# SSD scan: output transposes one period behind the norm, step-size transposes behind the fifth unit, four output rows split ahead of the last unit

## The chip, the core and the metric

The kernel runs on one core of a Trainium2 chip. A core has TensorE (PE in the profile) for matmuls and transposes, VectorE (DVE), ScalarE (ACT) and GpSimd (POOL) for elementwise work, and SyncE (SP), whose queue issues every transfer of this kernel. Each engine takes its instructions strictly in the order in which they stand in its queue, and waits at each one until its semaphores allow it. The metric is the device time of one execution in microseconds (us); lower is better.

## What is computed

The program is a stack of layers over 1024 tokens of width 1024. The change lies in the second mixer, a state space layer (SSD), and in the layernorm behind it:

```
z, xbc, dt = split(x @ w_in)                     # 2048 + 3072 + 32 columns
xbc = silu(causal_conv4(xbc));  xs, B, C = split(xbc)      # 4 groups, state 128
dt = softplus(dt + dt_bias);  a = -exp(a_log)
cs = cumsum(dt * a) in chunks of 128 tokens
y_diag = ((C B^T) * exp(cs_l - cs_s), lower triangle) @ (xs * dt)
state  = B^T (xs * dt * exp(cs_end - cs)), carried from chunk to chunk
y = y_diag + (C @ state) * exp(cs) + d_skip * xs
y = rmsnorm over a group of 512 of (y * silu(z)), * norm_w
out = y @ w_out                                  # 2048 -> 1024
x = layernorm(sqrt2 * x + out);  then rmsnorm(x) feeds the feed-forward layer
```

All matmuls take fp32 operands split in a high and a low part (`whi`, `wlo`; `x` holds both parts of the activations), three products for each.

## The kernel before, in words

The SSD layer's input projection is cut into four groups of ten units on TensorE. In a group, units 0 and 1 (`states`) give B and C, units 2 to 5 (`inputs`) give x, 48 matmuls of 128x512 each (L174); units 6 to 9 (`gates`) give z, 96 matmuls of 128x256 (L860 to L862). A unit's weights come by one or two transfers into `wst` (L156), are rounded to `whi` on ScalarE (L140) and completed by `wlo` on VectorE (L141). Behind the first six units the result goes through a causal convolution: ScalarE copies it out of PSUM (L331, L332), VectorE adds three taps (L334).

The scan of group g runs while the units of group g+1 run: behind each of its first eight units stands one chunk of 128 tokens (`chunk(n)`, n = 8g to 8g+7), that of the last group behind the eight tiles of the output projection. I call a unit with its chunk a period. A chunk is
- `heads(n)`: eight small matmuls (L916), their sum on VectorE (L917);
- `between(n)`: the carried state (L925, L930, L926 to L933); the transfer of the gate values into `xw` (L936);
- `within(n+1)`: the next chunk's decay matrix `s` (transfer L897, GpSimd L898, VectorE L899, ScalarE L900, VectorE L909), B C^T (L902, L903), and three products on GpSimd (L906 to L908);
- `finish(n-1)`: the gate product (L941), the sum of squares (ScalarE L943), the inverse root in nine small VectorE steps (tiles `rs`, L259 to L269), the scaling (ScalarE L945), four transposes into PSUM (L948), the copy out (ScalarE L949) and the transfer to memory (L950).

Ahead of the first group stand the step sizes: `lead` (L191) multiplies the dt columns and the first unit together, `softplus` and the cumulative sum run on VectorE (to L796), and seven TensorE instructions (L807 to L812) turn the result round for the scan.

Behind the fourth group `SsdOut` computes y @ w_out. `fill(k)` loads, scales and splits one of 16 rows of w_out (L1003, ScalarE L1005, VectorE L1006). `early(i)` multiplies rows 8, 9 and 0 to 7 for token tile i (60 matmuls, L668); `rest()` multiplies the other six rows (36 matmuls) and runs the layernorm (L1066, then L653 to L659) and the next layer's rmsnorm (L1081 to L1091) on the tile. Each second tile `ops.build` transposes both tiles (16 transposes, L1137) and forms the operands of the feed-forward layer, whose matmuls are L1230.

What sets the order: the Tile framework schedules instructions into the engines' queues from the order in which they are written and from its own costs. `turn()` is `issue_after(anchor(K))`: what is written in it stands behind the last TensorE instruction written so far. Buffers are rings: two for `wst`, four each for `whi` and `wlo` (the copy `raw` for the convolution takes one of the `wlo` ring too), two for the large PSUM tiles `pa`, four for the small ones `pb`. A tile takes the slot of the one as many allocations before it, and waits until that one's last reader is done.

## Time and profile before

| | |
|---|---|
| three runs, median (lowest to highest) | 3383.68 us (3379.7 to 3386.35) |
| profiled execution: its time, its span | 3383.42 us, 3381.6 us |
| mean granted TensorE clock | 0.963 |
| busy: PE, DVE, ACT, POOL | 3093.0 (91%), 2281.6 (67%), 1623.7 (48%), 779.2 us (23%) |

The profiled execution lies 0.26 us from the median, so its rows can be read for the median. 1.8 us of its time lie outside the span. A row of the timeline gives start, duration, engine, line of the program, operation, what it writes and reads by tile name, and in brackets how long the engine had been idle before it and what ended that. The granted clock of TensorE has two levels in these rows, 1.00 (2.4 GHz) and 0.50 (1.2 GHz).

### The profile page before, as it was taken

What the parts mean: (1) busy time and instruction counts of PE and PEld (TensorE: products, weight loads), DVE (VectorE), ACT (ScalarE), POOL (GpSimd) and SP (SyncE); (2) the same over time, 40 slices, a digit from 0 to 9 for tenths busy, and PEclk for the clock granted to TensorE, in tenths of its full rate; (3) what the DMA queues carried; (4) which work ended last, traced back from release to release, by engine and by line L of the source; (5) the groups of instructions that cost most, each with busy time, mean ns of one, the idle gap of its engine ahead of it and who ended that gap; (6) DMA issues with size and microseconds to landing.
All of it is one profiled execution on the core that took longest, in us unless ns stands there. A gap on an engine that the chain in (4) does not pass through costs nothing. (4 is left out here: it accounts for less than half of the span.)

```text
span 3381.6 us, 42341 instructions
## 1 busy us (share of the span) xinstructions
PE 3093.0 (91%) x15560; PEld 2582.5 (76%) x15560; DVE 2281.6 (67%) x3819; ACT 1623.7 (48%) x2943; POOL 779.2 (23%) x487
## 2 busy tenths in 40 slices
PE   8999996999999889878999989899999699999997
PEld 6878875878787867667778877678787588888776
DVE  6537775366657555888785689835676955555998
ACT  5526533345545532465555434542475665554442
POOL 0000011113232211532233345100000423232543
PEclk9999998999999999989999999999999899999999
DMA  3257342233343555323332620435453422224322
GB/s 126 66 198 222 105 142 66 63 82 103 88 115 82 141 177 159 102 77 131 112 116 85 213 83 22 156 126 211 137 154 127 163 75 78 90 76 142 113 81 112
DMA packets 344960, 398.99 MB, mean 118 GB/s; under 512 B 20656, under 2 KB 270640, under 8 KB 344752
## 3 DMA queue, kind: packets, MB, share of 16 engines
q1 hardware_dynamic: 344752, 396.28, 37.5%
q8 instruction: 123, 2.02, 0.2%
q14 instruction: 85, 0.70, 0.1%
HBM read 279.29 MB, written 116.92 MB: 117 GB/s over the span
## 5 line engine op out<-in xcount | busy, mean ns | idle before, releaser
L141 DVE TENSOR_TENSOR wlo<-wst,whi 128x1024 fp32r<-128x1024 f32 (+1 forms) x190 | 225.5, 1190 | 338.9 <-ACT whi L140 338.7
L174 PE MATMUL pa<-x,whi 128*128 128x512 f32 x1568 | 430.5, 396 | 5.2 <-ACT l L332 2.7
L140 ACT ACTIVATE whi<-wst 128x1024 fp32r<-128x1024 f32 (+1 forms) x190 | 180.0, 949 | 355.9 <-PE pa L174 94.0
L174 PEld LDWEIGHTS pa<-x,whi 128*128 128x128 f32 x1568 | 294.3, 189 | 69.8 <-issue 3.4
L147 ACT ACTIVATE wst<-wst,pk 128x128 f32<-128x128 f32 (+1 forms) x816 | 251.5, 391 | 177.8 <-DMA wst<-in_ffn_w_in_dram 105.6
L174 PE MATMUL pa<-x,wlo 128*128 128x512 f32 x784 | 244.1, 393 | 1.8 <-DVE wlo L141 1.8
L1230 PE MATMUL pa<-x,whi 128*128 128x512 f32 (+1 forms) x736 | 222.6, 385 | 6.3 <-DVE rl L264 3.2
L1230 PE MATMUL pb<-x,whi 128*128 128x512 f32 (+1 forms) x736 | 224.0, 381 | 0.0
L1309 PE MATMUL pa<-wlo,whi 128*128 128x512 f32 x768 | 190.9, 407 | 15.5 <-DVE wlo L141 13.3
L1309 PE MATMUL pb<-wlo,whi 128*128 128x512 f32 x744 | 180.1, 400 | 13.8 <-DVE wlo L141 13.8
L1309 PEld LDWEIGHTS pa<-wlo,whi 128*128 128x128 f32 x768 | 151.0, 198 | 52.9 <-DVE wlo L141 17.7
L1193 POOL TENSOR_TENSOR s<-wst 128x512 f32<-128x512 f32 x44 | 57.6, 1310 | 570.7 <-ACT wst L147 532.0
L1309 PEld LDWEIGHTS pb<-wlo,whi 128*128 128x128 f32 x744 | 143.1, 193 | 46.6 <-DVE wlo L141 16.7
L174 PEld LDWEIGHTS pa<-x,wlo 128*128 128x128 f32 x784 | 148.0, 189 | 34.0 <-DVE wlo L141 2.2
L1230 PEld LDWEIGHTS pa<-x,whi 128*128 128x128 f32 x736 | 137.7, 192 | 34.1 <-issue 3.6
L1230 PEld LDWEIGHTS pb<-x,whi 128*128 128x128 f32 x736 | 135.8, 188 | 26.5 <-issue 0.4
L898 POOL TENSOR_TENSOR s<-s,p 128x1024 f32<-128x1024 f32 x32 | 63.8, 1995 | 382.5 <-DMA s<-d 382.5
L860 PE MATMUL pa<-whi,x 128*128 128x256 f32 x512 | 148.7, 290 | 1.6 <-ACT l L332 1.3
L861 PE MATMUL pa<-wlo,x 128*128 128x256 f32 x512 | 147.4, 288 | 0.0
L862 PE MATMUL pa<-whi,x 128*128 128x256 f32 x512 | 147.4, 288 | 0.0
L140 ACT ACTIVATE whi<-s 128x1024 fp32r<-128x1024 f32 x88 | 93.1, 1058 | 108.2 <-POOL s L1194 53.1
L1230 PE MATMUL pa<-x,wlo 128*128 128x512 f32 (+1 forms) x368 | 141.2, 385 | 0.1
(580 smaller groups left out, 8021.6 us busy)
## 6 DMA issues: line engine op xcount, KB each, us to landing
wst<-in_ffn_w_in_dram SPq DMA_DIRECT2D x88, 512.0 KB, 3.8
d<-l SPq DMA_DIRECT2D x83, 512.0 KB, 3.3
d<-p SPq DMA_DIRECT2D x82, 512.0 KB, 3.3
x<-d SPq DMA_DIRECT2D x128, 256.0 KB, 5.4
p<-d SPq DMA_DIRECT2D x46, 512.0 KB, 5.0
wst<-in_s_w_in_dram SPq DMA_DIRECT2D x40, 512.0 KB, 4.0
s<-d SPq DMA_DIRECT2D x32, 512.0 KB, 9.9
l<-d SPq DMA_DIRECT2D x24, 512.0 KB, 5.6
```

The lines of the kernel that those rows point to most:

```text
L140: K.nc.scalar.activation(hi, src, AF.Copy)
L141: (eng or K.nc.vector).tensor_tensor(lo, src, hi.bitcast(F32), ALU.subtract)
L147: K.nc.scalar.activation(st[:, k, :], st[:, k, :], AF.Copy, scale=col(K, gain, k0 + k))
L174: K.nc.tensor.matmul(ps[:, h:h + 512], w, x[:, h:h + 512], start=k == 0 and m == 0, stop=k == n - 1 and m == 2)
L860: nc.tensor.matmul(o, xh, wh, start=k == 0, stop=False)
L861: nc.tensor.matmul(o, xh, wl, start=False, stop=False)
L862: nc.tensor.matmul(o, xl, wh, start=False, stop=k == NK - 1)
L898: nc.gpsimd.tensor_tensor(mv, mv, per_head(csT, P), ALU.subtract)
L1193: G(s1, a21, a22, ALU.add)
L1230: nc.tensor.matmul(p, l[:, k, :], r[:, k, :], start=k + m == 0, stop=k == 3 and m == 2)
L1309: nc.tensor.matmul(bank[j], th[:, a + o:a + o + P], tw[:, b:b + 512], start=c + m == 0, stop=c == n - 1 and m == 2)
```

## The change

Five things are different.
1. The seven TensorE instructions of the step sizes and the copies behind them become a function `steps()`, called behind unit 4 of the first group.
2. `finish(n)` is cut in two. `norm(n)` stays where it was, one period behind its chunk. `flip(n)` (the transposes, the copy, the transfer to memory) goes one period later, to the head of `chunk(n+2)`; the copy goes into `xw` and no longer into `xdt`. On GpSimd the product `y` goes ahead of `xw`. A group's last two flips stand behind its units 8 and 9 (`close`), those of the last group behind the first two tiles of `rest`. `within` of a group's first chunk stands behind unit 8 and no longer behind unit 9.
3. Rows 8, 9, 0 and 1 of w_out are filled in `ahead()`, written behind unit 7 of the last group; rows 0 and 1 lie in two tiles `p` and no longer in `x`.
4. In `rest` each tile's matmuls are written under `issue_after` of the last TensorE instruction.
5. `rest` drives the last group's `close`.

```diff
@@ -801,17 +801,19 @@
         sl = slice(128 * c, 128 * c + 128)
         nc.scalar.activation(w2[:, sl], cs[:, sl], AF.Exp, bias=cs[:, 128 * c + 127:128 * c + 128], scale=-1.0)
     nc.vector.tensor_tensor(w2, w2, dt, ALU.mult)
-    b, b2 = K.B(), K.B()
-    for c in range(2):
-        sl = slice(128 * c, 128 * c + 128)
-        nc.tensor.transpose(b[:, 128 * c:128 * c + 128], dt[:, sl], K.ident)
-        nc.tensor.transpose(b[:, 256 + 128 * c:384 + 128 * c], cs[:, sl], K.ident)
-        nc.tensor.transpose(b2[:, 128 * c:128 * c + 128], w2[:, sl], K.ident)
-    nc.vector.tensor_copy(sf[:, 0:512], b)
-    nc.vector.tensor_copy(w2T, b2[:, 0:256])
-    nc.tensor.matmul(b2[:, 256:512], sel, csT, start=True, stop=True)
-    nc.scalar.activation(ecs, csT, AF.Exp)
-    nc.scalar.activation(cdb, b2[:, 256:512], AF.Exp)
+
+    def steps():
+        b, b2 = K.B(), K.B()
+        for c in range(2):
+            sl = slice(128 * c, 128 * c + 128)
+            nc.tensor.transpose(b[:, 128 * c:128 * c + 128], dt[:, sl], K.ident)
+            nc.tensor.transpose(b[:, 256 + 128 * c:384 + 128 * c], cs[:, sl], K.ident)
+            nc.tensor.transpose(b2[:, 128 * c:128 * c + 128], w2[:, sl], K.ident)
+        nc.vector.tensor_copy(sf[:, 0:512], b)
+        nc.vector.tensor_copy(w2T, b2[:, 0:256])
+        nc.tensor.matmul(b2[:, 256:512], sel, csT, start=True, stop=True)
+        nc.scalar.activation(ecs, csT, AF.Exp)
+        nc.scalar.activation(cdb, b2[:, 256:512], AF.Exp)
 
 
 
@@ -904,8 +906,8 @@
         nc.vector.tensor_tensor(cbm, b[:, 0:128], tri, ALU.mult)
         nc.scalar.activation(bt, b[:, 128:256], AF.Copy)
         nc.gpsimd.tensor_tensor(hv(xdt), hv(X), per_head(dtT, 64), ALU.mult)
+        nc.gpsimd.tensor_tensor(hv(y), hv(X), dsk[:, 8 * g:8 * g + 8].unsqueeze(2).to_broadcast([P, 8, 64]), ALU.mult)
         nc.gpsimd.tensor_tensor(hv(xw), hv(X), per_head(w2T, 64), ALU.mult)
-        nc.gpsimd.tensor_tensor(hv(y), hv(X), dsk[:, 8 * g:8 * g + 8].unsqueeze(2).to_broadcast([P, 8, 64]), ALU.mult)
         nc.vector.tensor_tensor(mv, mv, cbm.unsqueeze(1).to_broadcast([P, 8, P]), ALU.mult)
         held[n] = mv, Cc, xdt, xw, y, bt
 
@@ -935,54 +937,75 @@
                 nc.vector.tensor_copy(prev, st)
         nc.sync.dma_start(xw, sz_d[g][c * P:(c + 1) * P, :])
 
-    def finish(n):
-        g, c = divmod(n, 8)
-        _, _, xdt, sz, y, _ = held.pop(n)
+    def norm(n):
+        _, _, xdt, sz, y, _ = held[n]
         nc.vector.tensor_tensor(y, y, sz, ALU.mult)
         t = K.small(2, "yss", bufs=3)
         nc.scalar.activation(xdt, y, AF.Square, accum_out=t[:, 0:1])
         rsqrt_col(K, t[:, 1:2], t[:, 0:1], 1, 1.0 / 512, 1e-6)
         nc.scalar.activation(y, y, AF.Copy, scale=t[:, 1:2])
+
+    def flip(n):
+        g, c = divmod(n, 8)
+        _, _, _, xw, y, _ = held.pop(n)
         yt = K.B()
         for q in range(4):
             nc.tensor.transpose(yt[:, q * P:(q + 1) * P], y[:, q * P:(q + 1) * P], K.ident)
-        nc.scalar.activation(xdt, yt, AF.Copy)
+        nc.scalar.activation(xw, yt, AF.Copy)
         nc.sync.dma_start(yd[4 * g:4 * g + 4, :, c * P:(c + 1) * P].rearrange("m p t -> p m t"),
-                          xdt.rearrange("p (m t) -> p m t", m=4))
+                          xw.rearrange("p (m t) -> p m t", m=4))
 
     def turn():
         return K.tc.issue_after(anchor(K))
 
     def chunk(n):
         with turn():
+            if n % 8 > 1:
+                flip(n - 2)
             heads(n)
             between(n)
             if n % 8 < 7:
                 within(n + 1)
             if n % 8:
-                finish(n - 1)
+                norm(n - 1)
+
+    def close(n):
+
+        with turn():
+            flip(n - 1)
+            norm(n)
+        yield
+        with turn():
+            flip(n)
+        yield
 
     for g in range(4):
+        end = close(8 * g - 1)
         for i, unit in enumerate(units(g)):
             with turn() if g + i else nullcontext():
                 unit()
+            if g == 0 and i == 4:
+                with turn():
+                    steps()
             if g and i < 8:
                 chunk(8 * g - 8 + i)
             if 3 <= i < 7:
                 with turn():
                     tokens(g, i - 3)
-            if g and i == 8:
-                with turn():
-                    finish(8 * g - 1)
-        with turn():
-            within(8 * g)
+            if i > 7:
+                if g:
+                    next(end)
+                if i == 8:
+                    with turn():
+                        within(8 * g)
+            if (g, i) == (3, 7):
+                out.ahead()
     out.prepare()
     for i in range(NT):
         with turn():
             out.early(i)
         chunk(24 + i)
-    with turn():
-        finish(31)
+    return close(31)
 
 
 class SsdOut:
@@ -1009,13 +1032,22 @@
     def half(self, i):
         return self.yh[:, 512 * (i % 2):512 * (i % 2) + 512]
 
+    def ahead(self):
+
+        K = self.K
+        self.an = [anchor(K)] * 2
+        with deferred(K, self.an[0]):
+            for k in (8, 9):
+                self.fill(k)
+            for k in (0, 1):
+                t = K.P2(F32R)
+                self.fill(k, t[:, 0, :], t[:, 1, :])
+
     def prepare(self):
         K = self.K
         self.an = [anchor(K)] * 2
         xw = [K.X() for _ in range(4)]
-        for k in (8, 9):
-            self.fill(k)
-        for k in range(8):
+        for k in range(2, 8):
             self.fill(k, xw[k // 4][:, k % 4, :], xw[2 + k // 4][:, k % 4, :])
         for k in (10, 11):
             self.fill(k)
@@ -1037,7 +1069,7 @@
         nc.vector.scalar_tensor_tensor(x, x, SQRT2, a, ALU.mult, ALU.add)
         nc.sync.dma_start(self.zd[i * P:(i + 1) * P, :], x)
 
-    def rest(self):
+    def rest(self, end):
 
         K, I, nc, w, ops = self.K, self.I, self.K.nc, self.w, self.ops
         for k in range(14, 16):
@@ -1061,8 +1093,10 @@
                 yv = dict(zip((10, 11), stream_rows(K, self.yd, 10, i, self.half(i), n=2)))
                 yv.update(zip(range(12, 16), stream_rows(K, self.yd, 12, i)))
                 nc.sync.dma_start(z, self.zd[i * P:(i + 1) * P, :])
-            out_tile(K, a, [w[k] for k in order], lambda k: yv[order[k]], 6)
+            with K.tc.issue_after(anchor(K)):
+                out_tile(K, a, [w[k] for k in order], lambda k: yv[order[k]], 6)
             an.append(anchor(K))
+            next(end, None)
             nc.vector.tensor_tensor(z, z, a, ALU.add)
             layernorm(K, z, g, b, i < 6)
             nc.sync.dma_start(self.x2[i * P:(i + 1) * P, :], z)
@@ -1879,8 +1913,7 @@
     yd = K.DR([16, P, T])
     ops = Ops(K)
     out_b = SsdOut(K, I, yd, x1, x2, ops)
-    ssd_layer(K, I, XT.get, yd, out_b)
-    out_b.rest()
+    out_b.rest(ssd_layer(K, I, XT.get, yd, out_b))
     XT = _Late(K)
 
     def done(i, x, y):
```

The first piece of the order is TensorE's queue in a column period of the third group, ahead of the change (`pb_6970` receives the transposes of one chunk, `pb_6923` is the sum of the next chunk's heads).

```order
2434 L174 MATMUL pa_6860<-x_3541,wlo_6863 128x512 x2
2435 L916 MATMUL pb_6923<-r_4327,s_6812 128x64 x8
2436 L925 MATMUL pb_6933<-p_4132,q_5136 128x512
2437 L930 MATMUL pb_6937<-r_4327 128x512
2438 L902 MATMUL pb_6947<-q_5136 128x128
2439 L903 MATMUL pb_6947<-ident,q_5136 128x128
2440 L948 MATMUL pb_6970<-ident,p_4329 128x128 x4
2441 L878 MATMUL pa_6977<-ident,l_6785 128x128 x8
2442 L174 MATMUL pa_6988<-x_3540,whi_6990 128x512 x2
```

With the change (lines are those of the changed kernel, so L953 is the flip, L918 the heads, L904 and L905 are B C^T, L880 is the transposes of x).

```order
2434 L174 MATMUL pa_6853<-x_3541,wlo_6856 128x512 x2
2435 L953 MATMUL pb_6916<-ident,r_4315 128x128 x4
2436 L918 MATMUL pb_6923<-r_4314,s_6812 128x64 x8
2437 L927 MATMUL pb_6933<-p_4132,q_5136 128x512
2438 L932 MATMUL pb_6937<-r_4314 128x512
2439 L904 MATMUL pb_6947<-q_5136 128x128
2440 L905 MATMUL pb_6947<-ident,q_5136 128x128
2441 L880 MATMUL pa_6970<-ident,l_6778 128x128 x8
2442 L174 MATMUL pa_6981<-x_3540,whi_6983 128x512 x2
```

The four transposes have moved from behind B C^T to ahead of the heads, and belong to a chunk one earlier.

The second piece is SyncE's queue around the last group's gates units, before: `wst_8699` and `wst_8705` are the weights of units 8 and 9, the transfers of L1003 are rows of w_out, `l_8495` is the result of unit 6.

```order
316 L156 DMA wst_8699<-in_s_w_in_dram 128x4x256
317 L897 DMA s_8517<-d_4302 128x8x128
318 L156 DMA wst_8705<-in_s_w_in_dram 128x4x256
319 L936 DMA r_4327<-d_4325 128x512
320 L950 DMA d_4130<-p_4329 128x4x128
321 L1003 DMA wst_8950<-in_s_w_out_dram 128x1024
322 L1003 DMA wst_8956<-in_s_w_out_dram 128x1024
323 L865 DMA d_4326<-l_8495 128x4x256
324 L897 DMA s_8932<-d_4302 128x8x128
```

With the change (L1026 is the row of w_out, L867 the result of a gates unit, `l_8653` that of unit 7, `l_8823` that of unit 8; `wst_8714` and `wst_8720` are the weights of units 8 and 9).

```order
322 L1026 DMA wst_8692<-in_s_w_out_dram 128x1024
323 L1026 DMA wst_8698<-in_s_w_out_dram 128x1024
324 L867 DMA d_4313<-l_8653 128x4x256
325 L955 DMA d_4130<-r_4314 128x4x128
326 L899 DMA s_9098<-d_4302 128x8x128
327 L1026 DMA wst_8705<-in_s_w_out_dram 128x1024
328 L1026 DMA wst_8710<-in_s_w_out_dram 128x1024
329 L156 DMA wst_8714<-in_s_w_in_dram 128x4x256
330 L156 DMA wst_8720<-in_s_w_in_dram 128x4x256
331 L1026 DMA wst_8972<-in_s_w_out_dram 128x1024
332 L1026 DMA wst_8976<-in_s_w_out_dram 128x1024
333 L867 DMA d_4313<-l_8823 128x4x256
```

The weights of units 8 and 9 stood ahead of unit 6's result and of all rows; they now stand behind unit 7's result and behind four rows. ScalarE's queue with the change shows the same place (L866 is the result of unit 7, L1028 a row of w_out, L140 the weights of units 8 and 9):

```order
682 L866 ACTIVATE l_8653<-pa_8556 128x1024
683 L954 ACTIVATE r_4314<-pb_8656 128x512
684 L1028 ACTIVATE whi_8693<-wst_8692,pk 128x1024
685 L1028 ACTIVATE whi_8699<-wst_8698,pk 128x1024
686 L944 ACTIVATE p_4316,yss_8834<-p_4316 128x512
687 L1028 ACTIVATE p_8704<-wst_8705,pk 128x1024
688 L946 ACTIVATE p_4316<-p_4316,yss_8834 128x512
689 L1028 ACTIVATE p_8709<-wst_8710,pk 128x1024
690 L902 ACT_TABLE_LOAD
691 L902 ACTIVATE s_9098<-s_9098 128x1024
692 L140 ACTIVATE whi_8715<-wst_8714 128x1024
693 L140 ACTIVATE whi_8721<-wst_8720 128x1024
```

Of these rows, the two for rows 8 and 9 stand behind unit 7's result, and the weights of units 8 and 9 are the last.

The third piece is TensorE's queue in `rest`, before: `pa_10327` and `pa_10447` are the fourth and the fifth tile, L1137 are the transposes of `build` for the first pair of tiles.

```order
3738 L668 MATMUL pa_10327<-whi_10026,s_10331 128x512
3739 L1137 MATMUL pb_10207<-ident,p_10036 128x128 x4
3740 L1137 MATMUL pb_10212<-ident,p_10036 128x128 x4
3741 L668 MATMUL pa_10327<-whi_10026,s_10331 128x512
3742 L668 MATMUL pa_10327<-wlo_10027,s_10331 128x512 x2
3743 L668 MATMUL pa_10327<-whi_10026,s_10331 128x512 x2
3744 L668 MATMUL pa_10447<-whi_8995,l_9007 128x512 x2
```

With the change (L1171 are the transposes of `build`, `pa_10112` is the second tile, `pa_10249` the third, L953 the last flip).

```order
3695 L668 MATMUL pa_10112<-whi_10000,s_10116 128x512 x2
3696 L953 MATMUL pb_10157<-ident,r_4315 128x128 x4
3697 L1171 MATMUL pb_10209<-ident,p_10010 128x128 x4
3698 L1171 MATMUL pb_10214<-ident,p_10010 128x128 x4
3699 L1171 MATMUL pb_10219<-ident,p_10010 128x128 x4
3700 L1171 MATMUL pb_10224<-ident,p_10010 128x128 x4
3701 L668 MATMUL pa_10249<-whi_8997,l_9009 128x512 x2
```

The transposes for the first pair stood inside the fourth tile's matmuls; they now stand directly behind the second tile, and the third tile stands behind all of them. The second and the third pair are in the same position now: two tiles, 16 transposes, two tiles. Behind the eighth tile stand 48 matmuls of the feed-forward layer, then the transposes of the fourth pair.

## Rows read from the trace of the kernel before

**Rows 1.** Timeline of PE, step sizes and first group; idle time and releaser in brackets.

```profile
568.82 0.45 PE L807 MATMUL pb<-ident,l 128*128 128x128 f32 x1 [16.98 <-DVE l L250]
...
627.00 1.20 PE L174 MATMUL pa<-x,whi 128*128 128x512 f32 x4 [1.33 <-ACT l L332]
```

**Rows 2.** Windows: length, then PE, PEld, DVE, ACT, POOL busy, PEclk, DMA share, GB/s.

```profile
568.00:576.00 8.00, 5.68 (x15) 3.92 (x16) 3.15 (x7) 1.49 (x4) 0.00 (x0) 0.50 0.18 52
```

**Rows 3.** Waits of PE, 700 to 1180 us: in total, times, longest.

```profile
PE pb L948 <- DVE r L917: 11.9, 8, 3.1
PE pb L948 <- ACT r L945: 8.0, 4, 3.2
PE pb L948 <- ACT p L945: 6.9, 2, 4.2
PE pb L948 <- DVE p L917: 5.5, 4, 2.1
```

**Rows 4.** Timeline of PE, one column period.

```profile
913.53 1.17 PE L174 MATMUL pa<-x,whi 128*128 128x512 f32 x4
...
924.54 1.89 PE L916 MATMUL pb<-r,s 128*128 128x64 f32 x16
...
929.12 0.63 PE L948 MATMUL pb<-ident,p 128*128 128x128 f32 x4 [0.59 <-DVE r L917]
```

**Rows 5.** Timeline of SP, the weight transfers of two column periods.

```profile
911.55 0.37 SPq L156 DMA_DIRECT2D wst<-in_s_w_in_dram  x1
...
928.40 0.37 SPq L156 DMA_DIRECT2D wst<-in_s_w_in_dram  x1
```

**Rows 6.** Timeline of PE, behind unit 7 of the second, third and fourth group.

```profile
825.14 0.70 PE L948 MATMUL pb<-ident,r 128*128 128x128 f32 x4 [3.21 <-ACT r L945]
...
985.42 0.66 PE L948 MATMUL pb<-ident,p 128*128 128x128 f32 x4 [4.22 <-ACT p L945]
...
1148.83 0.65 PE L948 MATMUL pb<-ident,r 128*128 128x128 f32 x4 [2.42 <-ACT r L945]
```

**Rows 7.** Timeline of ACT, last group, behind unit 7.

```profile
1148.68 1.14 ACT L1005 ACTIVATE whi<-wst,pk 128x1024 fp32r<-128x1024 f32 x1
...
1151.13 1.02 ACT L864 ACTIVATE l<-pa 128x1024 f32<-128x1024 f32 x1
```

**Rows 8.** Timeline of DVE, same place.

```profile
1153.22 1.28 DVE L1006 SCALAR_TENSOR_TENSOR wlo<-wst,pk,whi 128x1024 fp32r<-128x1024 f32 x1 [0.84 <-ACT whi L1005]
```

**Rows 9.** Transfers issued at 1154.54 us: KB each, us to landing.

```profile
wst<-in_s_w_out_dram SPq DMA_DIRECT2D x1, 512.0 KB, 10.7
```

**Rows 10.** Page, part 6, transfers of the whole run: KB each, median us to landing.

```profile
wst<-in_s_w_in_dram SPq DMA_DIRECT2D x40, 512.0 KB, 4.0
```

**Rows 11.** Waits of PE, 1180 to 1345 us, output tiles of `early`.

```profile
PE pb L948 <- DVE r L917: 11.5, 4, 5.5
...
PE pb L948 <- DVE p L917: 3.0, 2, 2.1
PE pa L668 <- DVE x L1006: 1.6, 3, 0.6
PE pa L668 <- ACT x L1005: 1.2, 1, 1.2
```

**Rows 12.** Timeline of DVE, layernorm of the first tile of `rest`, its start.

```profile
1355.65 1.21 DVE L1066 TENSOR_TENSOR p<-p,pa 128x1024 f32<-128x1024 f32 x1
```

**Rows 13.** Timeline of ACT, the same tile, its end.

```profile
1374.80 1.16 ACT L1091 ACTIVATE p<-p,pns 128x1024 f32<-128x1024 f32 x1 [2.57 <-DVE pns L269]
```

**Rows 14.** Waits of PE, 1345 to 1470 us, `rest` and the first feed-forward matmuls.

```profile
PE pb L1137 <- ACT p L1091: 23.5, 5, 9.6
PE pa L1230 <- DVE rl L264: 3.2, 1, 3.2
PE pa L1230 <- DVE wlo L141: 2.7, 1, 2.7
```

**Rows 15.** Timeline of PE, feed-forward layer.

```profile
1547.33 1.19 PE L1230 MATMUL pa<-r,whi 128*128 128x512 f32 x2 [6.22 <-DVE p L1478]
```

## Prediction

> **What bounds the kernel now.** I read the page's first part (TensorE is busy nine tenths of the span, no other engine more than seven), then TensorE's waits stretch by stretch, then the timelines of the engines that end those waits. TensorE is the bound, so a gain is an idle stretch that it loses, and a loss is one that the change puts in. Five places have idle time that the change touches. At the step sizes TensorE stands 16.98 us for the softplus on VectorE [rows 1], and the clock is still at 0.50 (1.2 GHz) after it [rows 2]. In the groups the transposes L948 wait 32.3 us in all (11.9 + 8.0 + 6.9 + 5.5) [rows 3]; among the tiles of `early` they wait 14.5 us, and splits of w_out hold the first tile 2.8 us [rows 11]. In `rest` and behind it the transposes of `build` and the first feed-forward matmuls wait 29.4 us [rows 14]. Behind unit 7 of the last group there is only 2.42 us of wait [rows 6]; I name it because the change works there too.
>
> **Step sizes: -23 us.** The seven instructions move behind unit 4, so the 16.98 us go, and with them the half-speed start of unit 1. What it leaves: from the end of `lead` (568.82 - 16.98 = 551.84) to the start of unit 5 (627.00 [rows 1]) before, 75.2 us. After: four units at 11.0 us (913.53 to 924.54 [rows 4]) make 44.0, one wait of 1.3 for the PSUM tile as now [rows 1], the sixteen transposes of x, the seven instructions and a copy between them 4.3 (estimated from their number and widths), and three waits for `wlo`, which VectorE now splits between softplus steps, of 0.5 us each: 51.1. That is 24 less; I take 23. Nobody needs the step sizes before the first chunk, five units later, and what is queued behind them on VectorE is units' work. If VectorE falls behind, the bound is the old wait back in smaller pieces: 18 to 25.
>
> **Flips in the column periods: +1.** In a column period TensorE waits at L948 because the slot of `pb` that the transposes want is still being read by L917, and L917 stands behind VectorE's `rs` steps and a weight split. These follow a circle without TensorE: a split frees `wst`, SyncE issues the next weights and behind them `s`, `s` lands, GpSimd and VectorE work on it, the `rs` steps follow, then the next split. SyncE issues L156 at 911.55 and 928.40 [rows 5], 16.85 us apart; TensorE waits 0.59 of that [rows 4], so its own work is about 16.3. The change leaves this circle alone. It moves the transposes ahead of the heads, so the wait at L948 goes, but the ring of `pb` has four slots as before and a period takes five: L902 now takes the slot that the flip has filled, and waits for the copy L949. ScalarE has that copy behind the convolution's L332, which in turn stands behind the scaling L945 at the end of the `rs` steps: as late in the circle as L917 was. So the wait changes its place and the period stays 16.85; I give half a microsecond a group for the phase. SyncE now has the flip's transfer ahead of the gate transfer L936, and GpSimd has `y` ahead of `xw`, which waits for that transfer: both have most of a period before L941 and L930 want them. If that is not enough, each of twelve periods gets longer. Bounds: -22 (all of 32.3 but the next paragraph's share) to +12.
>
> **Flips behind unit 7: -8 us.** Here L948 waited 3.21, 4.22 and 2.42 us for the norm of the chunk just before [rows 6]. One period later that norm is long done, and L902 doesn't occur in a group's last chunk. The first two are 7.4 us, with some half-speed time behind them; unit 9's result on ScalarE, still behind `s`, takes a little back. The third lies in the next paragraph but one.
>
> **Flips in `early`: -12 us.** L948 waits 14.5 us there [rows 11]. ScalarE has no convolution in these periods, so L949 runs early and L902 finds its slot. The longest wait, 5.5, keeps about half (2.5): the next tile's operands are split late in that period anyway. **A rule against it:** the Trainium skill, page "Perfetto Trace Analysis", section "Identifying Performance Opportunities", says that the same gap repeating on the engine that should be saturated can mean that there are too few buffers for the next tile. The column periods agree: L948's waits end with the reader of a slot [rows 3]. By that rule the gap would come back at L902 in `early` as well, since no slot is added, and this paragraph would be 0. I weigh it as a rival below.
>
> **Rows split ahead: +23 us.** The order decides here. Rows 8 and 9 take the two `whi` slots that units 8 and 9 used before, so their weights must wait until unit 7 has read its own, and they stand behind four rows in the two-slot ring of `wst`. Before, L948 ended its wait at 1148.83 [rows 6] and unit 8 began at 1149.3 with its weights in place. After, on ScalarE: the result of unit 7 ends at 1152.15 less the 1.14 of the row that stood ahead of it, 1151.0; row 8 takes 1.14 and on VectorE 1.28 [rows 7, 8], to 1153.4; only then `wst` is free for row 0. Its transfer stands behind `s` as one did at this place before, 10.7 us [rows 9], to 1164.1; the split 2.4, to 1166.5; only then the weights of units 8 and 9 can be fetched, 4.0 us [rows 10], to 1170.5; their split another 2.4, to 1172.9. Unit 8 starts 23.6 us later. The clock will be at half speed for some microseconds behind such a stop, as in [rows 2], +2; and the first output tile's 2.8 us of waits for splits [rows 11] go. 23.6 + 2 - 2.8 = 22.8. Bounds: if row 0's transfer also takes 4.0, 16; if the second transfer is as slow as the first, 29.
>
> **`rest`: +30 us.** Before, a pair's `build` stood inside or behind later tiles, so a layernorm had 8 to 16 us of matmuls to hide under, and still TensorE waited. Now the queue is two tiles, 16 transposes, two tiles, and nothing stands between the second tile and the transposes of it. How long the tile takes: from L1066 at 1355.65 [rows 12] to the end of L1091 at 1375.96 [rows 13], 20.3 us for the first tile, the one with the least company. The last flip and the transposes of the pair's first tile hide 1.4. So three stops of 18.9, 56.7 us. The fourth `build` has 48 matmuls, 11 us, ahead of it, and waits some 8. Together 64.7 against 29.4 now [rows 14]: +35.3. VectorE works on through the stops, so the feed-forward layer meets less of a backlog: 6.2 us of wait at 1547.33 [rows 15], of which I count 5 as saved. Stops of 15 would make it +18.6; stops of 25, with the stalls that neighbours cause now, +48.6.
>
> **Sum.** -23 + 1 - 8 - 12 + 23 + 30 = +11 us on the profiled 3383.4: 3394 us. That execution is 0.3 us from the median, so it stands for the median too. About 0.2%, 6.8 us, is what a measurement of this kernel can tell from no change.
>
> **Rivals.**
> - *The circle gives way* (ends on the other side). If the column periods fall to TensorE's own 16.3 us and the gap doesn't return at L902, all 22.4 us of L948 in the groups that I left (32.3 - 9.9) go: 3394 - 23 = 3371. It speaks for it that the waits are named after L917 and not after `s`; against it that the circle closes over SyncE, `s` and the splits with no TensorE instruction in it [rows 5]. It decides from 18 us of gain on.
> - *The gap comes back everywhere* (the change then doesn't do what its second edit says). L902 waits in `early` as L948 did: 3394 + 12 = 3406. For it: no slot more. Against: L949 has little ahead of it on ScalarE there.
> - *Short stops in `rest`.* With VectorE and GpSimd free of the third and fourth tile the layernorm takes 16.4 instead of 20.3 us, the stops are 15, and the loss is 18.6: 3394 - 12 = 3382, no change. Against: the 20.3 us are those of the tile that met the least of it.
>
> **How the numbers follow.** Forecast 0.45 (itself spread over some 12 us either way by the bounds of the two stops), the circle 0.15, the gap everywhere 0.13, short stops 0.17, anything else 0.10. Slower by over 0.2% (above 3390): most of the first and the whole of the third, 0.57. Within 0.2%: the rest of the first and most of the fourth, 0.21. Faster: the second, and part of the last two, 0.22. The range 3368 to 3416 reaches from the second to past the third and leaves out the double misses on either side. The forecast's own range is 3382 to 3406.
>
> **What would show it.** Right: no idle time between `lead` and unit 1, and unit 5 near 603; L902 waiting for L949 in the column periods with L156 still near 16.85 us apart; no wait behind unit 7 in the second and third group; one stop of over 20 us ahead of unit 8 of the last group, ended by L140 or L141 of its weights; three stops of 15 to 20 us ahead of the transposes of `build`, ended by L1091. Wrong: column periods at 16.3 us; unit 8's weights in place (then the +23 falls, and the sum is a gain); stops in `rest` under 13 us (the same); or a stop in a place that I gave nothing, such as L930 for `xw`.

## The result, and the profile after

The changed kernel takes 3410.8 us (median of four runs, 3406.03 to 3413.0); the kernel before took 3383.68 us beside it. The ratio is 1.0079, 95% interval 1.0062 to 1.0097: 27 us slower. The prediction was 3394 us in a range of 3368 to 3416, with slower as the likeliest sign. The profiled execution of the changed kernel is the fastest of the four, 3406.03 us, 4.8 us under the median. Its span and busy times by the page are:

```profile
span 3404.3 us, 42306 instructions
...
PE 3083.8 (91%) x15560; PEld 2575.4 (76%) x15560; DVE 2276.9 (67%) x3819; ACT 1626.3 (48%) x2945; POOL 770.9 (23%) x487
```

Nothing in these shares shows a change. What shows it is the start of the same TensorE instruction in the two timelines, place by place (us; the last column is how much the stretch since the row above gained or lost):

| place | before | after | shift | stretch |
|---|---|---|---|---|
| heads of chunk 0 | 699.18 | 672.44 | -26.74 | step sizes -26.7 |
| heads of chunk 7 | 819.12 | 793.08 | -26.04 | column periods +0.7 |
| heads of chunk 8 | 861.84 | 830.87 | -30.97 | behind unit 7 -4.9 |
| heads of chunk 15 | 978.39 | 951.89 | -26.50 | column periods +4.5 |
| heads of chunk 16 | 1022.10 | 990.07 | -32.03 | behind unit 7 -5.5 |
| heads of chunk 23 | 1143.60 | 1117.01 | -26.59 | column periods +5.4 |
| first matmul of unit 8 | 1149.24 | 1146.14 | -3.10 | rows ahead +23.5 |
| heads of chunk 24 | 1199.48 | 1192.76 | -6.72 | start of the output -3.6 |
| heads of chunk 31 | 1341.94 | 1329.70 | -12.24 | `early` -5.5 |
| wait in the feed-forward layer | 1547.33 | 1575.77 | +28.44 | `rest` +40.7 |
| end of the span | 3381.62 | 3404.3 | +22.7 | behind it -5.7 |

The last row is not the change's: behind 1640 us all kernels of this study run the same code, and each came out 0 to 7 us shorter there than the profiled run of before. So the +28.4 of the row above is what answers to the 27 us of the medians.

**Step sizes.** TensorE's timeline has no stop there any more [rows 1]; the moved instructions take 2.4 us, 1.06 of it a wait:

```profile
597.09 0.27 PE L809 MATMUL pb<-ident,l 128*128 128x128 f32 x1
...
598.97 0.70 PE L814 MATMUL pb<-p 128*128 128x256 f32 x2 [1.06 <-DVE p L813]
599.50 1.04 PE L880 MATMUL pa<-ident,l 128*128 128x128 f32 x8
600.30 1.17 PE L174 MATMUL pa<-x,whi 128*128 128x512 f32 x4
```

Unit 5 starts at 600.30, not 627.00.

**Flips.** TensorE's waits in the groups (673 to 1120 us) are two rows; L904 is the B C^T product (L902 before), L954 the flip's copy (L949 before):

```profile
PE pb L904 <- ACT r L954: 16.8, 7, 4.4
PE pb L904 <- ACT p L954: 9.3, 4, 3.6
```

The transposes wait no more, the product behind them does: 26.1 us. Of the 32.3 us of before [rows 3] 9.9 stood behind units 7 [rows 6], so it is the 22.4 us of the column periods that have become 26.1, in stops of up to 4.4 us where they were 3.1 at most. The waits are only part of the loss there. Column periods of the third group, before and then after (length, then PE, PEld, DVE, ACT, POOL busy, PEclk, DMA share, GB/s):

```profile
861.84:978.39 116.55, 110.71 (x648) 93.87 (x647) 89.48 (x139) 65.36 (x83) 35.81 (x22) 1.00 0.42 104
```

```profile
830.87:951.89 121.02, 114.02 (x649) 96.10 (x647) 89.43 (x139) 65.20 (x83) 34.02 (x23) 0.97 0.40 98
```

TensorE is busy 3.3 us longer with the same number of matmuls, at a lower granted clock: behind the stop of 3.28 us in this stretch it reads 0.78 (868 to 873 us). Over the three groups idle time grows by 3.8 us and busy time by 6.8, together the 10.6 us of the table.

Among the tiles of `early` the product waits too, 8.7 us in three stops. The longest, in TensorE's timeline, and ScalarE's ahead of it (L946 is the scaling at the end of the norm):

```profile
1234.95 0.49 PE L904 MATMUL pb<-q 128*128 128x128 f32 x2 [3.99 <-ACT r L954]
```

```profile
1232.87 0.72 ACT L946 ACTIVATE r<-r,yss 128x512 f32<-128x512 f32 x1 [2.18 <-DVE yss L269]
...
1234.32 0.57 ACT L954 ACTIVATE r<-pb 128x512 f32<-128x512 f32 x1
```

The flip's first transpose stands at 1226.86. Its copy runs at 1234.32, since it stands in ScalarE's queue behind the scaling of the next chunk's norm and two splits (L140).

**Rows ahead.** TensorE's timeline at unit 8, then SyncE's of the weight transfers ahead of it (L1026 rows of w_out, L156 the unit's own weights), then the transfers issued from 1105 to 1150 us (KB each, median us to landing):

```profile
1146.14 0.58 PE L862 MATMUL pa<-whi,x 128*128 128x256 f32 x1 [26.32 <-ACT whi L140]
1147.40 0.58 PE L863 MATMUL pa<-wlo,x 128*128 128x256 f32 x1 [0.68 <-DVE wlo L141]
```

```profile
1107.52 4.39 SPq L1026 DMA_DIRECT2D wst<-in_s_w_out_dram  x2
1128.19 2.14 SPq L1026 DMA_DIRECT2D wst<-in_s_w_out_dram  x2
1141.27 1.92 SPq L156 DMA_DIRECT2D wst<-in_s_w_in_dram  x2
```

```profile
wst<-in_s_w_out_dram SPq DMA_DIRECT2D x6, 512.0 KB, 10.2
wst<-in_s_w_in_dram SPq DMA_DIRECT2D x2, 512.0 KB, 4.2
```

Rows 0 and 1 are issued from 1128.19 on, behind a transfer of `s`, and take 10 us; their splits free `wst`, the unit's weights follow at 1141.27 and take 4, their split ends the stop at 1146.14. From 3 us into the stop to 7 us behind its end the granted clock is 0.50 (1.2 GHz):

```profile
1123.00:1153.00 30.00, 6.18 (x27) 5.88 (x28) 12.30 (x19) 14.12 (x15) 4.21 (x3) 0.50 0.57 149
```

**`rest`.** The transposes of the four builds (L1171) in TensorE's timeline, and the wait in the feed-forward layer that answers to [rows 15]:

```profile
1368.01 1.97 PE L1171 MATMUL pb<-ident,p 128*128 128x128 f32 x8 [18.21 <-ACT p L1125]
1374.03 1.97 PE L1171 MATMUL pb<-ident,p 128*128 128x128 f32 x8 [4.05 <-ACT p L1125]
1408.87 1.97 PE L1171 MATMUL pb<-ident,p 128*128 128x128 f32 x8 [15.14 <-ACT p L1125]
1413.58 1.97 PE L1171 MATMUL pb<-ident,p 128*128 128x128 f32 x8 [2.73 <-ACT p L1125]
1447.71 1.97 PE L1171 MATMUL pb<-ident,p 128*128 128x128 f32 x8 [15.36 <-ACT p L1125]
1452.41 1.97 PE L1171 MATMUL pb<-ident,p 128*128 128x128 f32 x8 [2.73 <-ACT p L1125]
1484.28 1.97 PE L1171 MATMUL pb<-ident,p 128*128 128x128 f32 x8 [6.17 <-ACT p L1125]
1491.77 1.97 PE L1171 MATMUL pb<-ident,p 128*128 128x128 f32 x8 [5.52 <-ACT p L1125]
...
1575.77 1.19 PE L1264 MATMUL pa<-r,whi 128*128 128x512 f32 x2 [6.10 <-DVE p L1512]
```

Each pair of tiles has two stops, one for each tile's scaling on ScalarE (L1125). The pairs make 22.3, 17.9, 18.1 and 11.7 us; all eight stops make 69.9 us where 29.4 us stood [rows 14].

### The profile page after: what moved, and what is told of

It is laid out like the page before. It is cut to its first block, busy times and chain, and to the rows that moved or that the text cites. A ratio compares the mean times of both kernels' runs of the same rounds, so it can differ in the third digit from the quotient of the medians.

```text
span 3404.3 us, 42306 instructions
## 1 busy us (share of the span) xinstructions
PE 3083.8 (91%) x15560; PEld 2575.4 (76%) x15560; DVE 2276.9 (67%) x3819; ACT 1626.3 (48%) x2945; POOL 770.9 (23%) x487
## 5 line engine op out<-in xcount | busy, mean ns | idle before, releaser
L140 ACT ACTIVATE whi<-wst 128x1024 fp32r<-128x1024 f32 (+1 forms) x190 | 180.0, 948 | 346.6 <-PE pa L174 94.9
L862 PE MATMUL pa<-whi,x 128*128 128x256 f32 x512 | 149.2, 291 | 27.9 <-ACT whi L140 26.3
L174 PEld LDWEIGHTS pa<-x,wlo 128*128 128x128 f32 x784 | 148.0, 189 | 33.7 <-DVE wlo L141 2.0
L1264 PEld LDWEIGHTS pb<-x,whi 128*128 128x128 f32 x736 | 136.2, 189 | 26.7 <-issue 0.4
L140 ACT ACTIVATE whi<-s 128x1024 fp32r<-128x1024 f32 x88 | 93.1, 1058 | 110.4 <-POOL s L1228 60.5
```

Of the source, the lines that this page charges most:

```text
L140: K.nc.scalar.activation(hi, src, AF.Copy)
L174: K.nc.tensor.matmul(ps[:, h:h + 512], w, x[:, h:h + 512], start=k == 0 and m == 0, stop=k == n - 1 and m == 2)
L862: nc.tensor.matmul(o, xh, wh, start=k == 0, stop=False)
L1264: nc.tensor.matmul(p, l[:, k, :], r[:, k, :], start=k + m == 0, stop=k == 3 and m == 2)
```

## The experiments

The theory: the two holds (rows ahead of unit 8, tiles behind `build`) lose more than the step sizes win, and the flips are worth little, since the ring of four PSUM tiles is short by one in any order. Every ratio below is to the kernel before, run beside it (3382.25 us for the first four runs, 3381.71 for the next four, 3381.22 for the last two); in brackets is the 95% interval.

**1. The hold in `rest` taken out of the change.**

```diff
-            with K.tc.issue_after(anchor(K)):
-                out_tile(K, a, [w[k] for k in order], lambda k: yv[order[k]], 6)
+            out_tile(K, a, [w[k] for k in order], lambda k: yv[order[k]], 6)
```

> The changed kernel, with the six output rows of the last pass no longer held behind the transposes of the build ahead of them. Theory A (the held rows make the three stops of 15 to 22 us and nothing else does): the stops before the build's transposes go back to 23.5, 3.2 and 2.7 us, the 37 us that the two traces show between the end of the early pass and the end of the builds come back, 3411 - 37 = 3374 us (3368 to 3382). Rival B (chunk 31's closing, now inside the last pass, stops TensorE there with or without the hold): half of it or less comes back, 3392 us or more.

Measured: 3370.98 us, ratio 0.9974 (0.9960 to 0.9988); 39.8 us less than the changed kernel. TensorE's waits from 1345 to 1500 us now begin with

```profile
PE pb L1170 <- ACT p L1124: 15.6, 3, 8.4
PE pa L1263 <- ACT whi L140: 5.2, 1, 5.2
PE pa L1263 <- DVE wlo L141: 4.7, 1, 4.7
PE pa L1263 <- DVE p L1268: 3.8, 1, 3.8
PE pa L668 <- DVE pns L1116: 2.7, 1, 2.7
```

There are 15.6 us at the build in place of 69.9. Some of that comes back as waits of the feed-forward layer (L1263): all waits of this stretch make 33.7 us in place of 70.1, a difference of 36.4. A is borne out, B falls.

**2. The rows ahead put back.** 

```diff
-            if (g, i) == (3, 7):
-                out.ahead()
...
-        for k in range(2, 8):
+        for k in (8, 9):
+            self.fill(k)
+        for k in range(8):
             self.fill(k, xw[k // 4][:, k % 4, :], xw[2 + k // 4][:, k % 4, :])
```

> The changed kernel, with the four output rows 8, 9, 0 and 1 filled where the kernel before fills them. Theory A (they delay the last unit's weights by what they take): the 26.3 us stop before unit 8 goes, the output pass waits some 3 us more at its start, net 20 us back, 3411 - 20 = 3391 us (3385 to 3397). Rival B (the splits cost ScalarE and VectorE the same wherever they stand, and the stop only moves to the start of the output pass): 3405 us or more.

Measured: 3394.96 us, ratio 1.0034 (1.0022 to 1.0046); 15.8 us less than the changed kernel, somewhat under the 20 of A and far from B's 6. Unit 8 starts without a stop, 29.2 us earlier, but at the heads of chunk 24 only 18.2 us of that are left. The first output tile waits

```profile
1152.39 1.22 PE L668 MATMUL pa<-whi,l 128*128 128x512 f32 x2 [10.61 <-ACT l L140]
```

against 4.82 us in the kernel before and 3.02 in the changed one, and splits of w_out hold it 2.3 us more. What it waits for are its rows of y (`l`). The first of their transfers in SyncE's timeline, in the kernel before and then in this run:

```profile
1171.18 1.88 SPq L681 DMA_DIRECT2D q<-d  x2
```

```profile
1143.62 1.89 SPq L681 DMA_DIRECT2D q<-d  x2
```

That is 27.6 and 28.9 us behind the heads of chunk 23 (1143.60, 1114.74), though unit 8 starts 5.6 us behind them before and 2.2 here. In both kernels these transfers stand in SyncE's queue behind unit 8's result, that stands on ScalarE behind the decay matrix `s` of the next chunk, and `s` is fetched behind unit 7's result, which ScalarE copies out 7.5 and 7.6 us behind the heads. The transposes behind unit 7 are not in this chain, so the tile starts no earlier behind the heads (36.0 us before, 37.7 here), and what unit 8 gains by its earlier start is waited at the tile. Why the rows of y are issued 1.3 us later stays open.

**3. Both undone:** the edits of runs 1 and 2 together.

> The changed kernel with both undone: rows free in the last pass, output rows filled as before. If the two parts are independent, 3411 - 37 - 20 = 3354 us (3347 to 3362): steps and later flips alone, 30 us faster than the kernel before. If the flips one period late are themselves a loss (chunk 31's closing in the last pass, the wait at the heads), it lies above the run with the step sizes alone.

Measured: 3357.34 us, ratio 0.9921 (0.9908 to 0.9935). The two parts add up: 39.8 + 15.8 = 55.6 by themselves, 53.5 together.

**4. The step sizes alone, in the kernel before.** The seven instructions and their readers become `steps()`, as in the change, and

```diff
+            if g == 0 and i == 4:
+                with turn():
+                    steps()
```

> The kernel before with one part of the change, the step-size transposes behind the fifth unit. The traces show chunk 0's heads 26.7 us earlier, 1.2 us of it from before: 3384 - 25.6 = 3358 us (3353 to 3363). If an earlier start were given back later (the weights of the later units set the pace), it would be 3370 us or more.

Measured: 3354.26 us, ratio 0.9915 (0.9902 to 0.9929): 28.0 us less than before, by the interval 24 to 33. Nothing is given back later. It also settles the flips: run 3 is this kernel with the flips and what goes with them (the order on GpSimd, the closing of the last group inside `rest`), and stands 3 us above it, with overlapping intervals. The flips, for which I had counted 19 us, bring no gain that can be measured.

**5. The flip behind the heads** (run 3 with two lines changed in order).

```diff
+            heads(n)
             if n % 8 > 1:
                 flip(n - 2)
-            heads(n)
```

> The run with both parts undone (3357 us), with the flip's four transposes issued behind the eight head matmuls instead of ahead of them. Theory C (a chunk takes five PSUM tiles from a ring of four, so the fifth always waits for the reader of the first): the waits of TensorE at the B-C product for the flip's copy (1 to 7 us, 22 us in all up to 1100 us and 10 us in the early pass) are replaced there by waits for the heads' add on VectorE of 0.6 to 2.7 us, as the transposes had in the kernel before; 3357 us or up to 8 us less. Rival D (the copy itself, late on ScalarE, is what holds TensorE, and nothing else): the waits at the B-C product go altogether, about 30 us less, 3327 us.

Measured: 3354.35 us, ratio 0.9919 (0.9906 to 0.9933). TensorE's waits from 690 to 1120 us, first of run 3, then of this run (L919 is the heads' add):

```profile
PE pb L904 <- ACT r L954: 17.7, 7, 4.1
PE pb L904 <- ACT p L954: 7.5, 2, 4.8
```

```profile
PE pb L904 <- DVE r L919: 13.3, 7, 2.7
PE pb L904 <- DVE p L919: 8.0, 4, 2.3
PE pb L904 <- ACT r L954: 4.7, 2, 3.0
PE pb L904 <- ACT p L954: 1.2, 1, 1.2
```

The place of the wait stays, most of it (21.3 of 27.2 us) now has the reader of the heads' tile as its releaser, which comes first in this order, and the sum hardly moves (25.2 to 27.2 us). That is C; D falls.

**6. Two rows ahead in place of four** (run 3 with `ahead` back at its place, filling rows 0 and 1 alone).

```diff
+            if (g, i) == (3, 7):
+                out.ahead()
```

> The run with both parts undone (3357 us), with only rows 0 and 1 filled ahead of the last unit, at the place of the change; rows 8 and 9, which take the slots of the weights' high halves, stay where the kernel before has them. Theory E (the transfers through the two-slot ring stand one behind the other, each pair some 10 us): half of the four rows' stop of 26.3 us stays before unit 8, 13 us, and some 5 us come back at the start of the output: 3365 us (3360 to 3370). Rival F (rows 8 and 9 cost, since they hold the slots that the last unit's weights need): no stop before unit 8, 3350 to 3357 us.

Measured: 3365.18 us, ratio 0.9958 (0.9944 to 0.9971), 8 us above run 3. The stop before unit 8, and the transfers issued from 1105 to 1150 us:

```profile
1140.92 0.58 PE L862 MATMUL pa<-whi,x 128*128 128x256 f32 x1 [19.80 <-ACT whi L140]
```

```profile
wst<-in_s_w_out_dram SPq DMA_DIRECT2D x5, 512.0 KB, 4.4
wst<-in_s_w_in_dram SPq DMA_DIRECT2D x2, 512.0 KB, 10.5
```

F falls: without rows 8 and 9 the stop is there. E's time came out, its stop did not: not half but three quarters of it, since now the unit's own weights stand behind a transfer of `s` and take 10.5 us in place of 4.2.

**7. The hold alone** (run 4 with the hold put in; chunk 31 closes ahead of `rest`).

```diff
-            out_tile(K, a, [w[k] for k in order], lambda k: yv[order[k]], 6)
+            with K.tc.issue_after(anchor(K)):
+                out_tile(K, a, [w[k] for k in order], lambda k: yv[order[k]], 6)
```

> The run with the step sizes alone (3354 us) and one line more: the output rows of the last pass held behind the transposes of the build ahead of them; chunk 31 closes ahead of the pass, as in the kernel before. Theory A (the hold alone makes the stops): three stops of 15 to 20 us, 35 to 40 us slower, 3390 us (3384 to 3397). Rival G (part of it is chunk 31's closing inside the pass): 20 us or less, below 3375 us.

Measured: 3400.05 us, ratio 1.0056 (1.0044 to 1.0069), 45.8 us above run 4. TensorE's waits from 1345 to 1500 us are one row:

```profile
PE pb L1142 <- ACT p L1096: 65.4, 8, 15.5
```

The hold makes the stops by itself, G falls. The time lies 3 us above the range that I had given: the hold costs 6 us more here than in the change, where the last two flips stand among the held tiles; whether that is why wasn't tried.

**8. Two rows behind unit 8** (run 4 with `ahead` for rows 0 and 1, one unit later than in the change).

```diff
+            if (g, i) == (3, 8):
+                out.ahead()
```

> The run with the step sizes alone (3354 us), with rows 0 and 1 filled behind unit 8 instead of at the start of the output: unit 9 needs no weights of its own, so the two-slot ring is free then. If the place is what cost in the change, no stop appears before unit 8, and the stop of 5.3 us before the first output tile shrinks: 3349 us (3346 to 3354). If something else holds that tile (rows 8 and 9, the rows of y), no change: 3354 us.

Measured: 3351.23 us, ratio 0.9910 (0.9897 to 0.9924), 3 us under run 4, which the intervals don't separate. Unit 8 has no stop, so the place was what cost; but the first output tile has a longer one, 15.05 us against 5.29 in run 4:

```profile
1157.60 1.22 PE L668 MATMUL pa<-whi,l 128*128 128x512 f32 x2 [15.05 <-ACT l L140]
```

The tile waits for its own rows of y (`l`). In SyncE's timeline four transfers of w_out rows now stand ahead of the last of them, which are issued at 1150.28; in run 4, with chunk 23 at the same time, at 1144.94. So the early fill brought the next rows of w_out forward too, ahead of the rows of y, and bought little.

**9. The flip in the other PSUM ring** (run 5 with one line changed).

```diff
-        yt = K.B()
+        yt = K.A()[:, 0:512]
```

> The run with the flip behind the heads (3354 us), with one line changed: the four transposes of the flip write to a tile of the other PSUM ring (two tiles of 1024, which the units' columns use), so that a chunk takes four tiles from the ring of four, not five. Theory C (the ring of four makes the wait): the waits at the B-C product go, about 25 us of them up to chunk 31; if the other ring has room, 3354 - 25 = 3329 us. If the two-tile ring is the next to be short, TensorE waits as long or longer ahead of the units and of the output tiles, and the time is 3354 us or more; theory C then still says that no wait stands at the B-C product. Rival H (the wait there is the chunk's own chain and not the ring): the waits at the B-C product stay as they are, 3354 us.

Measured: 3387.35 us, ratio 1.0019 (1.0009 to 1.0030), 33 us above run 5. TensorE's waits from 690 to 1345 us:

```profile
PE pa L862 <- ACT l L866: 29.1, 6, 6.2
PE pa L668 <- DVE l L1058: 13.3, 4, 7.5
PE pa L174 <- ACT l L332: 9.3, 3, 3.9
PE pa L880 <- ACT l L866: 6.0, 3, 2.9
PE pa L880 <- ACT l L332: 5.5, 3, 2.7
```

No row has L904: with four tiles on the ring of four its wait is gone altogether. Every wait is now at `pa`, the ring of two, 29.1 us of it ahead of the matmuls of units 8 and 9 (L862). C is borne out and H falls: periods without any stop of TensorE, such as those from 754.12 and from 926.12 us, have no wait at L904 either. PSUM has no tile to spare in either ring.

**10. The builds one pair later, no hold** (run 4 with the first three builds issued a pair of tiles later).

```diff
             if i % 2:
-                ops.build(zt[:, 0, :], z, i // 2)
+                late.append((zt[:, 0, :], z, i // 2))
+                if i > 1:
+                    ops.build(*late.pop(0))
```

(and the last one behind the eighth tile.)

> The run with the step sizes alone (3354 us), with each of the first three builds of the last pass issued one pair of tiles later, and no hold. If TensorE's stops of the last pass (some 25 us in that run, ended by the normed tile) are a matter of how many matmuls stand between a tile and the transposes of it, two tiles more (17 us) cover most of them: 3354 - 15 = 3339 us (3334 to 3348). If VectorE's work for the layernorms and the builds is what the feed-forward layer waits for, the wait moves there: 3354 us or more.

Measured: 3360.3 us, ratio 0.9931 (0.9916 to 0.9946), 6 us above run 4, with overlapping intervals. TensorE's waits from 1345 to 1500 us begin with

```profile
PE pb L1146 <- ACT p L1100: 21.4, 6, 8.0
PE pa L1239 <- DVE p L1071: 8.3, 1, 8.3
```

and in run 4 with

```profile
PE pb L1141 <- ACT p L1095: 20.9, 5, 8.8
```

My expectation failed: the builds wait as long as before (21.4 against 20.9 us), and one wait for VectorE comes in the feed-forward layer. The two timelines say why the edit did little: of the 288 matmuls of `rest` (L668), 144 stand ahead of the first eight transposes, 181 ahead of the next eight and 216 ahead of the next sixteen; in run 4 these are 139, 168 and 216. With builds and tiles free to pass each other the framework had put the transposes that late already. So this run doesn't show what more distance in TensorE's queue would be worth.

## Why the prediction was right in sum and wrong in some of its terms

| term | predicted | in the two traces | by runs |
|---|---|---|---|
| step sizes | -23 | -26.7 | -28.0 (run 4) |
| flips: columns, unit 7, `early` | +1, -8, -12 | +10.6, -10.5, -5.5 | +3 (run 3 less run 4) |
| rows ahead | +23 | +23.5 - 3.6 | +15.8 (run 2), +13.6 (run 3 against 1) |
| `rest` | +30 | +40.7 | +39.8 (run 1), +37.6 (run 3 against 2), +45.8 (run 7) |

- **Step sizes.** Right in mechanism and in size. From the end of `lead` to the start of unit 5 TensorE takes 50.7 us (549.58 to 600.30); 51.1 were predicted, and it took 75.2 before. Of the 26.7 us in the table 2.3 stand ahead of that stretch already (`lead` ends at 549.58 and not at 551.84), and 1 is what I took off the 24 that I had worked out.
- **Flips in the column periods.** The step "so the wait changes its place and the period stays" is right in its first half, and runs 5 and 9 bear that out; the copy stands where I had put it, behind L332 and the scaling (1023.92, 1025.45 and 1026.54 us for scaling, L332 and copy of one period). The second half failed: L156 of the third group is issued 16.9, 17.4 and 17.3 us apart, before 16.8, 16.7 and 16.9, and the loss is +10.6 us and not +1, near the bound of +12. The term left out that longer stops also lower the granted clock: 3.8 us are more waiting, 6.8 are slower matmuls. What makes the stops longer wasn't tried apart, neither SyncE's queue, from which I had argued the bound, nor the copy's place on ScalarE. With the flip behind the heads (run 5) the same stretches lose 6.5 us in all, in run 3 11.0, and with the step sizes alone (run 4) 0.7.
- **Flips behind unit 7.** Right for the second and third group: -10.5 by the traces for -8. Behind unit 7 of the last group nothing is won, since the first output tile's rows of y come no earlier for it (run 2).
- **Flips in `early`.** This step failed: "L949 runs early and L902 finds its slot". The copy runs late, behind the scaling of the next norm and two splits in ScalarE's queue (1234.32 us for transposes at 1226.86), and L904 waited 8.7 us (3.99 + 2.22 + 2.48) where L948 had waited 14.5 [rows 11]; the expected rest was 2.5. So the rival "gap comes back everywhere" held for about half of it. The rule weighed there (the Trainium skill, "Perfetto Trace Analysis", "Identifying Performance Opportunities": a repeating gap can mean too few buffers) agrees with run 9: one tile less on the ring takes the gap away, 0 us at L904.
- **Rows ahead.** Right at unit 8: 23.5 us later by the traces, 23.6 predicted, with the chain of the paragraph (two transfers of 10 and 4 us with their splits). Too large as a loss. From the heads of chunk 23 to those of chunk 24 the changed kernel takes 75.7 us, run 2 59.9 and the kernel before 55.9: the rows cost 15.9, near the 13.6 and 15.8 of the runs, and the other 4.0 come with the flips. What the sum lacked is that without the rows the first output tile waits 10.6 us for its rows of y, so that part of the stop at unit 8 is no additional loss.
- **`rest`.** Right in mechanism, 10 us too small. I counted one stop a pair and 64.7 us in all; the trace has two a pair and 69.9. And the 5 us that I credited to the feed-forward layer did not come: the wait there is 6.10 us, before 6.22 [rows 15]. These two make the whole difference.
- **Rivals.** The circle did not give way: the column periods got longer. Stops of 15 us were nearly there (15.14, 15.36 behind the first pair's 18.21), but with the second stop of each pair the sum is that of the forecast.

So the sign came from the two holds, as predicted, and the sum was 16 us low (27 against 11). By the runs the flips account for 22 of that and `rest` for 10, against 5 from the step sizes and 7 to 9 from the rows; that makes 18 to 20, 2 to 4 us more than the whole, which the medians don't resolve. That the errors have both signs is luck: the flips alone, for which 19 us of gain were counted and none came, are larger than the whole error. Versions without the holds beat both kernels: the step sizes alone at 3354.26 us, with the flip behind the heads 3354.35, with two rows behind unit 8 3351.23, all three within each other's intervals.

## What to carry to other kernels

Count the tiles that a period takes from a ring: here, with five on a ring of four, a wait moved off one tile came back at the next in both orders that were tried, and one tile less removed it (run 9), at the price of waits on the ring that took the tile. Before you move a copy, look at what stands ahead of it in its engine's queue. An order constraint that puts TensorE's next independent work behind a result still in the making costs most of the latency of that result; work that is loaded early must not stand ahead of a transfer that the next unit needs, in the queue or in a shared staging ring. Where a change has several parts, undo each by itself: here one part was worth 28 us and was buried under two that lost 55.

## What the runs showed of the hardware

- Two 512 KB transfers of a unit's weights landed in 3.7 and 4.6 us when `s` had landed before they were issued (changed kernel, 1141.27 us), and in 10.7 and 10.3 us when they were issued just behind the 512 KB transfer of `s`, which took 11.2 itself (run 6, 1129.05 us). In the changed kernel it is rows of w_out that stand at this place, and they took 10.5 and 9.9. So what stands ahead in the queue sets it, and not the kind of weights.
- In the changed kernel the granted clock fell to 0.50 (1.2 GHz) in the long stops of TensorE and was still there for the first instructions behind them: 1123 to 1153 us read 0.50 for the stop before unit 8, 7 us of it behind the stop's end, and 1355 to 1378, 1396 to 1416 and 1437 to 1457 us read 0.50 for the stops of the first three builds.
